# Order of the closing stage of an encoder layer: residuals, reciprocals, splits and closing sums of the output projection

## The chip, the cores and the metric

The kernel runs on one core of one Trainium2 chip. A core has five engines that work from queues of their own: TensorE (PE: matmuls, and PEld: its weight loads), VectorE (DVE), ScalarE (ACT), GpSimd (POOL) and SyncE (SP, which here only issues DMAs). The metric is the device time of one execution in microseconds (us), the median of several runs.

## The reference

One encoder layer over 2048 positions of width 1024, in float32. One input projection feeds two groups: a gated linear attention (width 512, scanned in both directions) and a latent attention with dense softmax (4 heads, width 512). Both are gated, put side by side, and go through one output projection; the result is added to the scaled input and normalised:

```python
    o_a = gla_branch(g_q, g_k, g_v, g_gate, g_lr_f, g_lr_b, wg2_f, bg_f, wg2_b, bg_b, gla_norm_g)
    o_b = mla_branch(m_cq, m_ckv, m_kr, m_gate, positions, q_norm_g, w_uq, kv_norm_g, w_ukv)
    return jnp.concatenate([o_a, o_b], axis=-1) @ w_out
...
        x = layer_norm(DEEPNORM_ALPHA * x + mixed, ln_g[layer], ln_b[layer])
```

## The kernel before

Every matrix product is made of three matmuls (`mm3`, L149 to L151): each operand is split into a high part (`hi`, L117, an ACT copy into the rounded type) and a low part (`lo`, L123, the difference, on VectorE or POOL); high times high, high times low and low times high are added up in PSUM.

The last stages are the dense attention and the output projection. The attention works through 16 blocks, 4 heads times 4 groups of 512 queries. A block ends with its row sums: `tot` brings them to SBUF, `tsum` transposes them on TensorE into a PSUM tile `sx` (L1103), `rcp` makes reciprocals `rc` of [128, 4], `keep` stores these to DRAM (`r_s`, L1115, a DMA from ACT's queue, one 4-byte element at a time), `oh` and `ol` split the block's output `o` into `ofh` and `ofl`, `y` multiplies it by the value weights, and `yc` stores that (`ob_s`). Only the last block (15) concerns us: its closing steps lie inside the output projection.

The output projection has 16 chunks of 128 positions. For a chunk c:

- `load`: four DMAs on SP of 256 KB each: the first group's half `of[:, 0]`, the gates `gr[:, 0]` (`gm_s`), the reciprocals broadcast over the partitions `gr[:, 1]` (`r_s`, L1309), and the second group's half `of[:, 1]` (`ob_s`, L1310). `load_res` fetches the residual input `xr` (512 KB, L1329).
- `split`: `hi` and `lo` of half 0 (tiles `oh`, `ol`), `gate` (two POOL multiplications of `of[:, 1]`, L1316), then `hi` and `lo` of half 1.
- `product`: two halves n of 512 output columns, each 8 steps k of three matmuls (24 matmuls); steps 0 to 3 use split half 0, steps 4 to 7 half 1. An odd chunk's two halves go into one PSUM tile of two banks (`po`, two such tiles in turn). An even chunk from 2 on has two tiles of one bank, `pmb` and `px`, one of each in the whole kernel; `px` takes its bank in turn with `sx` and `y`.
- `residual` of half n on VectorE: `rr` = alpha times `xr` plus the PSUM half (L1360), then its statistics (L1361). `finish`: mean and variance (L1369, L1370), a multiplication (L1372), the inverse root with two tiny ACT steps (`ln_l`, `ln_y`, L160 and L161) and four tiny VectorE steps (`ln_t`, `ln_r`, L162 to L165), a last multiplication (L1375), and the stores of the two halves to the output (L1376).

Dependencies are tracked by tile: a matmul into the second bank of `po` waits for a read of its first bank that was traced before it.

What sets the order: up to chunk 3's first work a list of places written out by hand orders all five engines (`in_order`, the dictionary `last`). For the rest, the loop over chunks 4 to 15 traces `load(c + 2)`, `split(c + 1)`, `load_res(c + 1)`, `product(c)` and `finish(c)`. There only SP keeps the traced order (`sp_order`, `SP_ONLY`), and the splits are only held behind the ends of the hand-written part (`ends`); the planner of the framework orders the other engines by its own costs. In the kernel before it put up to eleven matmuls of the following even chunk between an odd chunk's two halves (none in chunk 15), and splits of a chunk ahead of the ln steps of the chunk two before it. Each DMA also waits for the one eight places before it among all DMAs of SP and ACT, by its semaphore.

Of the kernel before, what the change touches and what calls it, by code (L numbers as in the profile page):

```python
# [18 lines left out]
P = 128  # L19
# [18 lines left out]
LATE_GATES = (NCH - 1, NCH - 2, 0)  # L38
STORE_POOL = (0, 1)
ENGINES = tuple(getattr(mybir.EngineType, n) for n in ("PE", "Activation", "DVE", "Pool", "SP"))  # L40
SP_ONLY = ENGINES[-1:]
RND = 1.5 * 2.0 ** 23


# [20 lines left out]
    tot=11.2,  # L65
    tsum=12.04,
    rcp=13.55,
    keep=14.21,
    oh=12.34,
    ol=12.99,  # L70
    y=16.55,
    yc=16.9,
# [36 lines left out]
class K:  # L109
# [856 lines left out]
    def attention(self):  # L966
        tc, nc = self.tc, self.nc
        mm = nc.tensor.matmul
        V, G, Ac = nc.vector, nc.gpsimd, nc.scalar
        NP = NKT // 2  # L970
        with ExitStack() as ctx:
# [6 lines left out]
            nb = len(blocks)  # L978
            stt = [dict(s=[None] * NP) for _ in blocks]
# [130 lines left out]
                V.reciprocal(rc, rc)  # L1110
                d["rc"] = rc

            def keep(i):
                h, b = blocks[i]
                Ac.dma_start(self.r_s[b][:, h].rearrange("o (e p) -> p (o e)", p=P), stt[i]["rc"])  # L1115

            def oh(i):
                d = stt[i]
# [30 lines left out]
            op = OutProj(self, ctx, qp, bp, sp, pS, pM, pX)  # L1149
# [8 lines left out]
            def at(f, i, j=None):  # L1158
                p = PLACE_LAST.get(f, PLACE[f]) if i == nb - 1 else PLACE[f]
                return p[j] if isinstance(p, tuple) else p  # L1160

            own = (("tot", tot), ("tsum", tsum), ("rcp", rcp), ("keep", keep), ("oh", oh), ("ol", ol), ("y", y), ("yc", yc))
            for i in range(nb):
                for j in range(NP):
# [42 lines left out]
            last = {}  # L1207
            for _, _, fn, a in sorted(todo, key=lambda e: e[:2]):
                with self.in_order(last):
                    fn(*a)  # L1210
            ends = [i for e, i in last.items() if e not in (mybir.EngineType.PE, mybir.EngineType.DVE)]


            late = dict(last)
            sp_order = lambda: self.in_order(late, SP_ONLY)
            rest = {c: o for c, o in enumerate(first)}

            def load(c):
                if c < NCH:
                    rest[c] = dict(c=c)  # L1220
                    op.load(rest[c])

            def split(c):
                if c < NCH:
                    with self.after(*ends):
                        for j in range(2):
                            op.hi(rest[c], j)
                            op.lo(rest[c], j)
                            if j == 0:
                                op.gate(rest[c])  # L1230

            with sp_order():
                load(4)
                for c in (2, 3):
                    op.load_res(rest[c])
                load(5)
                for c in (0, 1):
                    op.finish(rest[c])
                split(4)
                op.load_res(rest[4])  # L1240
                for c in (2, 3):
                    op.residual(rest[c], 0)
                    op.residual(rest[c], 1)
                    op.finish(rest[c])
            for c in range(4, NCH):
                with sp_order():
                    load(c + 2)
                    split(c + 1)
                    if c + 1 < NCH:
                        op.load_res(rest[c + 1])  # L1250
                    op.product(rest[c])
                    op.finish(rest[c])
                with self.after(*last.values()), sp_order():
                    for f in {4: (tot, tsum), 5: (rcp, keep, oh, ol), 6: (y,), 7: (yc,)}.get(c, ()):
                        f(nb - 1)


class OutProj:
# [88 lines left out]
    def product(self, o):  # L1347
        for n in range(2):
            for k in range(NK):
                self.part(o, k, (n,))  # L1350
            self.residual(o, n)


    def residual(self, o, n):
# [90 lines left out]
```

## Time and profile before

| | us |
|---|---|
| median of three runs | 1397.35 |
| the runs | 1395.38 to 1397.39 |
| the profiled execution | 1396.22 |
| its span, first to last instruction | 1394.4 |
| TensorE busy in the span | 1318.6 (95%) |
| VectorE busy | 1012.8 (73%) |
| ScalarE busy | 825.9 (59%) |
| GpSimd busy | 725.1 (52%) |

The page's second part cuts the span into 40 slices of 34.9 us, with the busy share in tenths. A row in order of time has the start, the duration, the engine, the line, the operation and the tiles; in square brackets stands the idle time ahead of it and what ended it. Matmuls are pipelined: a row's duration is longer than the step to the next row. A row of groups has a count behind `x`, busy time, mean, and the idle time before. `SPq` and `ACTq` are the queues in which DMAs are issued; "to landing" is the time from a DMA's issue to the arrival of its data.

### The profile page before, as it was taken

To read this page: it belongs to the slowest core of one execution; us is meant where nothing else is said; L and a number is where in the kernel's file an instruction comes from. 1 tells how busy PE (TensorE), PEld (TensorE's weight loads), DVE (VectorE), ACT (ScalarE), POOL (GpSimd) and SP (SyncE) were. 2 spreads that over 40 slices of the span, in tenths; PEclk is the share of its full clock that TensorE was granted. 3 is DMA by queue.
4 is the path that set the end of the run, shared out by engine and by line. 5 is a ranking of instruction groups with operands and counts; after the bars stand their busy time and mean duration, and the time that the engine had idled before them with its cause. 6 is when DMAs were issued, how large, how long until landed. Compare 5 with 4: busy or idle time off the path is not lost.

```text
span 1394.4 us, 19845 instructions
## 1 busy us (share of the span) xinstructions
PE 1318.6 (95%) x7056; PEld 1141.4 (82%) x7056; DVE 1012.8 (73%) x1829; ACT 825.9 (59%) x1353; POOL 725.1 (52%) x394
## 2 busy tenths in 40 slices
PE   7899999999989999999999999999999999988997
PEld 6799999999878888888778888888888887766775
DVE  7757755545598777777598888888888888384675
ACT  6655556555565555555487878788888887311110
POOL 3532423232342222221087888889999999734441
PEclk9999999999999999999999999999999999999999
DMA  7222223222565555552701111111133112465452
GB/s 248 80 74 64 68 69 91 69 69 68 179 236 165 169 179 167 167 167 93 224 0 39 39 38 38 39 53 61 54 84 84 45 31 34 141 192 161 162 187 100
DMA packets 108915, 147.38 MB, mean 106 GB/s; under 512 B 17838, under 2 KB 63278, under 8 KB 108816
## 3 DMA queue, kind: packets, MB, share of 16 engines
q1 hardware_dynamic: 99696, 143.98, 34.1%
q0 software_dynamic: 672, 2.10, 0.4%
q10 hardware_dynamic: 8448, 0.03, 0.3%
q8 instruction: 56, 0.92, 0.3%
q14 instruction: 43, 0.35, 0.1%
HBM read 94.93 MB, written 51.15 MB: 105 GB/s over the span
## 4 chain that ended last, share of the span: by engine, by line
PE 44%; DVE 12%; DMA 6%; ACT 3%; issue 2%; SPq 1%; POOL 1%; DVEq 0%; POOLq 0%; ACTq 0%
PE o L149 4%; PE o L150 4%; PE o L151 4%; PE pS L1000 4%; PE pS L1003 4%; PE pS L1002 4%; PE pS L1004 4%; PE pS L1001 4%; DMA xr<-x_dram 2%; DVE MMb L123 2%; DMA of<-ob_s 1%; PE po L149 1%; PE po L150 1%; PE ipm L149 1%; PE po L151 1%
## 5 line engine op out<-in xcount | busy, mean ns | idle before, releaser
L123 POOL TENSOR_TENSOR pl<-s,ph 128x1024 fp32r<-128x1024 f32 x128 | 307.1, 2414 | 66.9 <-ACT ph L117 60.4
L1022 DVE TENSOR_TENSOR rm<-pS,rm 128x512 f32<-128x512 f32 x210 | 144.9, 690 | 44.5 <-ACT s L1009 39.4
L1009 ACT ACTIVATE s<-pS 128x1024 f32<-128x1024 f32 x128 | 131.3, 1027 | 67.4 <-PE pS L1004 64.9
L1046 DVE TENSOR_TENSOR s<-s,mb 128x1024 f32<-128x1024 f32 x128 | 151.2, 1213 | 9.2 <-PE mb L1040 9.2
L117 ACT ACTIVATE ph<-s 128x1024 fp32r<-128x1024 f32 x128 | 135.1, 1057 | 16.7 <-PE o L151 16.1
L1050 ACT ACTIVATE s<-s 128x1024 f32<-128x1024 f32 x128 | 131.4, 1050 | 13.5 <-DVE s L1046 13.4
L149 PE MATMUL ipa<-wah,xah 128*128 128x384 f32 (+1 forms) x384 | 130.9, 341 | 6.0 <-ACT wah L117 6.0
L151 PE MATMUL ipa<-wah,xal 128*128 128x384 f32 (+1 forms) x384 | 126.1, 328 | 0.0
L150 PE MATMUL ipa<-wal,xah 128*128 128x384 f32 (+1 forms) x384 | 125.5, 327 | 0.2 <-DVE wal L123 0.2
L645 POOL TENSOR_TENSOR Us<-Us,cw 128x512 f32<-128x512 f32 x16 | 18.2, 1137 | 199.4 <-DVE Us L642 170.1
L1000 PE MATMUL pS<-qh,ckvT_h 128*128 128x512 f32 x256 | 103.9, 406 | 2.6 <-ACT s L1009 1.9
L149 PE MATMUL o<-ph,vh 128*128 128x512 f32 x256 | 102.6, 401 | 0.0
L151 PE MATMUL o<-ph,vl 128*128 128x512 f32 x256 | 101.3, 396 | 0.0
L1003 PE MATMUL pS<-rh,krs 128*128 128x512 f32 x256 | 101.2, 395 | 0.0
L150 PE MATMUL o<-pl,vh 128*128 128x512 f32 x256 | 101.1, 395 | 0.0
L1002 PE MATMUL pS<-qh,ckvT_l 128*128 128x512 f32 x256 | 100.8, 394 | 0.0
L1004 PE MATMUL pS<-rl,krs 128*128 128x512 f32 x256 | 100.7, 393 | 0.0
L1001 PE MATMUL pS<-ql,ckvT_h 128*128 128x512 f32 x256 | 100.7, 393 | 0.0
L117 ACT ACTIVATE oh<-of 128x512 fp32r<-128x512 f32 x32 | 20.0, 629 | 126.6 <-POOL of L1316 92.4
L1073 DVE TENSOR_TENSOR ap<-ap,s 128x512 f32<-128x512 f32 x120 | 83.1, 692 | 6.4 <-ACT s L1050 4.5
L149 PEld LDWEIGHTS ipa<-wah,xah 128*128 128x128 f32 x384 | 73.7, 192 | 6.8 <-ACT wah L117 6.0
L150 PEld LDWEIGHTS ipa<-wal,xah 128*128 128x128 f32 x384 | 74.0, 193 | 1.3 <-DVE wal L123 0.6
(319 smaller groups left out, 3932.0 us busy)
## 6 DMA issues: line engine op xcount, KB each, us to landing
xcf<-xT_dram SPq DMA_DIRECT2D x16, 512.0 KB, 4.3
xr<-x_dram SPq DMA_DIRECT2D x16, 512.0 KB, 5.5
out_dram<-rr SPq DMA_DIRECT2D x32, 256.0 KB, 2.0
xaf<-xT_dram SPq DMA_DIRECT2D x14, 512.0 KB, 4.2
SU<-su_s SPq DMA_DIRECT2D x16, 256.0 KB, 3.6
qdb<-qd_s SPq DMA_DIRECT2D x16, 256.0 KB, 4.2
oib<-oi_s SPq DMA_DIRECT2D x16, 256.0 KB, 2.7
ub<-u_s SPq DMA_DIRECT2D x16, 256.0 KB, 3.0
```

The costliest lines, as they stand in the source:

```text
L117: return nc.scalar.activation(dst, src, AF.Copy).ins
L123: return e.tensor_tensor(dst, src, hi.bitcast(F32), ALU.subtract).ins
L149: mm(out, ah, bh, start=start, stop=False)
L150: mm(out, ah, bl, start=False, stop=False)
L151: mm(out, al, bh, start=False, stop=stop)
L1000: mm(ps[:, e], kh, qh, start=True, stop=False)
L1001: mm(ps[:, e], kh, ql, start=False, stop=False)
L1002: mm(ps[:, e], kl, qh, start=False, stop=False)
L1003: mm(ps[:, e], kr, rh, start=False, stop=False)
L1004: mm(ps[:, e], kr, rl, start=False, stop=True)
L1022: V.tensor_tensor(d["rm"], src[:, e], d["rm"], ALU.max)
L1046: V.tensor_tensor(s, s, d["mb"][:, None, :].to_broadcast([P, 2, QB]), ALU.subtract)
```

## The change

Four things change in the output projection:

- In an odd chunk both residuals are traced behind both halves. Even chunks stay as they were.
- The order of ACT, POOL and SP is the traced one from the hand-written part to the end (`LATE_ORDER`); the splits are no longer held behind `ends`.
- The last block's closing steps are traced elsewhere: `tot`, `oh`, `ol` after chunk 4, `tsum` and `rcp` after chunk 5, `y` and `yc` after chunk 7.
- The last block's reciprocals are stored in four DMAs of 128 elements, after chunks 6, 7, 8 and 9. The other blocks' stores stay whole.

```diff
-SP_ONLY = ENGINES[-1:]
+LATE_ORDER = ENGINES[1], ENGINES[3], ENGINES[4]
...
-            def keep(i):
+            def keep(i, e=None):
                 h, b = blocks[i]
-                Ac.dma_start(self.r_s[b][:, h].rearrange("o (e p) -> p (o e)", p=P), stt[i]["rc"])
+                es = slice(0, 4) if e is None else slice(e, e + 1)
+                Ac.dma_start(self.r_s[b][:, h].rearrange("o (e p) -> p (o e)", p=P)[:, es], stt[i]["rc"][:, es])
...
-            ends = [i for e, i in last.items() if e not in (mybir.EngineType.PE, mybir.EngineType.DVE)]
...
-            sp_order = lambda: self.in_order(late, SP_ONLY)
+            fixed = lambda: self.in_order(late, LATE_ORDER)
...
             def split(c):
                 if c < NCH:
-                    with self.after(*ends):
-                        for j in range(2):
-                            op.hi(rest[c], j)
-                            op.lo(rest[c], j)
-                            if j == 0:
-                                op.gate(rest[c])
+                    op.hi(rest[c], 0)
+                    op.lo(rest[c], 0)
+                    op.gate(rest[c])
+                    op.hi(rest[c], 1)
+                    op.lo(rest[c], 1)
...
-                with self.after(*last.values()), sp_order():
-                    for f in {4: (tot, tsum), 5: (rcp, keep, oh, ol), 6: (y,), 7: (yc,)}.get(c, ()):
+                with self.after(*last.values()), fixed():
+                    for f in {4: (tot, oh, ol), 5: (tsum, rcp), 7: (y, yc)}.get(c, ()):
                         f(nb - 1)
+                    if 6 <= c < 10:
+                        keep(nb - 1, c - 6)
...
         for n in range(2):
             for k in range(NK):
                 self.part(o, k, (n,))
-            self.residual(o, n)
+            if o["c"] % 2 == 0:
+                self.residual(o, n)
+        if o["c"] % 2:
+            self.residual(o, 0)
+            self.residual(o, 1)
```

In the changed program TensorE does the two halves of an odd chunk without other matmuls between them, `sx` behind chunk 5 and `y` behind chunk 7; ACT does, from chunk 4 on, the two splits of chunk c + 1, then the ln steps of chunk c.

More of the change, by code (lines that the diff above doesn't have):

```diff
@@ L1224, in split @@
                 if c < NCH:
-                    with self.after(*ends):
-                        for j in range(2):
-                            op.hi(rest[c], j)
-                            op.lo(rest[c], j)
-                            if j == 0:
-                                op.gate(rest[c])
-            with sp_order():
+                    op.hi(rest[c], 0)
[3 more added lines that the diff above has]
+                    op.lo(rest[c], 1)
+            with fixed():
                 load(4)
@@ L1245, in attention @@
             for c in range(4, NCH):
-                with sp_order():
+                with fixed():
                     load(c + 2)
```

## The prediction

> **What bounds the kernel now.** I read the page first (busy shares, the 40 slices), then TensorE's rows in order of time from the last attention product to the end, then the waits, the DMA landings and the other engines' rows around TensorE's gaps.
>
> ```profile
> PE 1318.6 (95%) x7056; PEld 1141.4 (82%) x7056; DVE 1012.8 (73%) x1829; ACT 825.9 (59%) x1353; POOL 725.1 (52%) x394
> PE   7899999999989999999999999999999999988997
> ```
>
> TensorE is the bound of the whole run; what is left to win in the last five slices, where the change works, is its gaps. All gaps from output chunk 4 on, and some rows around them:
>
> ```profile
> 1227.31 0.39 PE L151 MATMUL po<-woh,ol 128*128 128x512 f32 x1
> 1229.78 0.47 PE L149 MATMUL pmb<-woh,oh 128*128 128x512 f32 x1 [2.09 <-DVE rr L1360]
> ...
> 1234.20 0.39 PE L149 MATMUL pmb<-woh,oh 128*128 128x512 f32 x1
> ...
> 1245.15 0.66 PE L1103 MATMUL sx<-ident,acc 128*128 128x128 f32 x4 [1.69 <-DVE rr L1360]
> ...
> 1259.79 0.80 PE L149 MATMUL po<-woh,oh 128*128 128x512 f32 x1 [6.65 <-DVE rr L1360]
> ...
> 1264.94 0.40 PE L149 MATMUL po<-woh,oh 128*128 128x512 f32 x1
> ...
> 1270.66 0.39 PE L149 MATMUL px<-woh,oh 128*128 128x512 f32 x1
> ...
> 1275.87 0.39 PE L151 MATMUL px<-woh,ol 128*128 128x512 f32 x1
> ...
> 1284.32 0.50 PE L149 MATMUL po<-woh,oh 128*128 128x512 f32 x1 [0.84 <-DVE rr L1360]
> ...
> 1289.67 0.39 PE L151 MATMUL po<-woh,ol 128*128 128x512 f32 x1
> ...
> 1308.65 0.50 PE L149 MATMUL po<-woh,oh 128*128 128x512 f32 x1 [2.27 <-DVE rr L1360]
> ...
> 1312.63 0.40 PE L150 MATMUL po<-wol,oh 128*128 128x512 f32 x1
> ...
> 1333.99 0.50 PE L149 MATMUL po<-woh,oh 128*128 128x512 f32 x1 [1.65 <-DVE rr L1360]
> ...
> 1357.80 0.50 PE L149 MATMUL po<-woh,oh 128*128 128x512 f32 x1 [1.74 <-DVE rr L1360]
> ...
> 1380.16 0.50 PE L149 MATMUL po<-woh,oh 128*128 128x512 f32 x1 [1.20 <-DVE rr L1360]
> ```
>
> There are eight gaps, and each ends on VectorE's residual (L1360). Six stand before a po matmul: the second half of chunks 5, 7, 9, 11, 13, 15, which waits until VectorE has read the first half of the same two-bank tile. Matmuls follow at (1275.87 - 1270.66) / 23 = 0.2265 us, though a row lasts 0.39; so a gap loses its listed idle time plus 0.16. A half-chunk (24 matmuls) takes 5.44 us, a chunk 10.87.
>
> **The change part by part.**
>
> *Residuals of odd chunks behind both halves.* The second half no longer waits. The six po gaps go: 6.65 + 0.84 + 2.27 + 1.65 + 1.74 + 1.20 = 14.35 listed. At the end of the run the first half's residual and statistics of chunk 15 now lie on the path, which they did not. An even chunk that did both at once shows their price:
>
> ```profile
> 1372.94 0.68 DVE L1360 SCALAR_TENSOR_TENSOR rr<-xr,pmb 128x512 f32<-128x512 f32 x1
> ...
> 1375.70 0.21 DVE L1369 BATCH_NORM_AGGREGATE mv<-bn 128x2 f32<-128x12 f32 x1
> ...
> 1385.95 0.69 DVE L1360 SCALAR_TENSOR_TENSOR rr<-xr,po 128x512 f32<-128x512 f32 x1 [5.11 <-PE po L151]
> ...
> 1387.40 0.21 DVE L1369 BATCH_NORM_AGGREGATE mv<-bn 128x2 f32<-128x12 f32 x1
> ```
>
> 2.76 us against 1.45: the tail grows by 1.31.
>
> *Closing sums later.* The transposes of the row sums (sx, L1103) stand in the middle of chunk 5's first half and wait 1.69 for VectorE to free their bank, which chunk 4's px holds. In the changed order they come after all of chunk 5, where that read is most of a chunk past: 1.69 goes. The product y, three matmuls, moves from chunk 7's first half to behind chunk 7; same work. The split ofh/ofl of the last block moves behind chunk 4's finish and takes 0.55 off VectorE ahead of chunk 2's residual (two starts below).
>
> *One order for ACT, POOL and SP.* ACT now runs the ln pair of chunk 1 ahead of the splits oh of chunk 4, where it stood behind them, and so on for each chunk. VectorE waited for it:
>
> ```profile
> 1221.50 0.63 DVE L123 TENSOR_TENSOR ofl<-o,ofh 128x512 fp32r<-128x512 f32 x1
> 1222.05 1.40 DVE L1375 SCALAR_TENSOR_TENSOR rr<-rr,ln_r,lnb 128x512 f32<-128x512 f32 x2
> ...
> 1228.05 1.00 DVE L162 TENSOR_TENSOR ln_t<-ln_y 128x1 f32<-128x1 f32 x1 [2.17 <-ACT ln_y L161]
> ...
> 1239.93 0.15 DVE L1370 TENSOR_SCALAR u<-mv 128x1 f32<-128x1 f32 x1
> ```
>
> Without the 2.17 and the 0.55, chunk 2's residual, which follows the row at 1228.05 and released chunk 4's first matmul, is done 2.7 us sooner: the gap of 2.09 at 1229.78 goes.
>
> Against this stands a new wait. ACT now does the splits of chunk 5 after the ln of chunk 3, and so after its u (1239.93 here), which in VectorE's new order has chunk 4's first residual ahead of it (0.6). u comes at 1239.93 - 2.17 - 0.55 + 0.6 = 1237.8. From u to the last split of chunk 5: ln 0.45, oh 0.63, ol 1.26, two gates 2.62, oh 0.63, ol 1.26, some 0.3 of hand-overs, 7.2 in all (rows below): done at 1245.0. TensorE without gaps starts chunk 5 at 1227.54 + 10.87 = 1238.4 and wants that split 14 matmuls later, at 1241.6. That is a wait of 3.4 at most; nothing at best, if VectorE, with the splits out of its way, closes up its 1228-1239 stretch by as much again. Between the ends I take 2.
>
> *Steps behind each other in the later chunks.* SP stays in order: chunk 10's loads stand behind chunk 7's stores. Nothing more is added to a queue than the three extra store parts on ACT (one issue each). The chain as it ran:
>
> ```profile
> 1297.95 1.00 SPq L1376 DMA_DIRECT2D out_dram<-rr  x2
> 1301.22 0.52 SPq L1310 DMA_DIRECT2D of<-ob_s  x1
> 1306.73 2.62 POOL L1316 TENSOR_TENSOR of<-of,gr 128x512 f32<-128x512 f32 x2 [2.16 <-DMA of<-ob_s]
> 1309.38 0.63 ACT L117 ACTIVATE oh<-of 128x512 fp32r<-128x512 f32 x1 [5.86 <-POOL of L1316]
> 1310.09 2.51 POOL L123 TENSOR_TENSOR ol<-of,oh 128x512 fp32r<-128x512 f32 x2 [0.74 <-ACT oh L117]
> ```
>
> Chunk 7 ended on TensorE at 1289.9; chunk 10's last split was done at 1311.4, that is 21.5 later. Without gaps TensorE wants it at 2 x 10.87 + 3.17 = 24.9 after chunk 7's end. Slack 3.4, or 2.1 with the odd chunk's finish 1.3 later: the loads stay hidden, cost nothing. If that cover goes, every us beyond it is TensorE's.
>
> *Reciprocals stored in four parts.* In the trace the whole store (512 elements of 4 bytes) sits in the worst place:
>
> ```profile
> DMA to landing us min/median/max: 8.2/8.3/9.2
> ...
> SPq L1309 <- DMA r_s<-rc: 6.2, 1, 6.2
> ...
> xr<-x_dram SPq DMA_DIRECT2D x1, 512.0 KB, 11.7
> of<-ob_s SPq DMA_DIRECT2D x1, 256.0 KB, 11.3
> ...
> of<-ob_s SPq DMA_DIRECT2D x13, 256.0 KB, 6.5
> ```
>
> (Landing of the reciprocal stores; SP's wait for one; chunk 5's residual input and chunk 6's ob load, issued in the same 0.7 us; the median of such loads.) SP stood 6.2 us for this store and the two loads beside it took 11 us instead of 6; the 6.65 us gap waited for that xr. With the store moved behind chunks 6 to 9 and cut in four, this place is free. A part is bounded by a quarter, 2.1, and the whole, 8.3; I take 3.7, a little over the quarter, as a load also has some fixed time. It delays its neighbours by at most 11.3 - 6.5 = 4.8 if it acts like the whole, by 1.2 if like a quarter; the latter stays inside the slack.
>
> *TensorE's clock.* After three of the gaps the matmuls run slowly: 12 steps from 1229.78 to 1234.20 take 4.42 where 2.72 is usual, 12 from 1259.79 to 1264.94 take 5.15, ten from 1308.65 to 1312.63 take 3.98 for 2.27. Excess 1.70 + 2.43 + 1.71 = 5.84, after waits of 2.09, 6.65 and 2.27; after 1.74 and less, none. I take it that the excess goes with the waits. The Trainium skill (TensorE: Matmul & The Clock Gate, "Why this matters for your kernels") puts the limit at idle gaps of about 3 us. By that rule two of the three stretches would have another cause and stay, and the sum would be smaller by 1.70 + 1.71 = 3.41. The rows speak for the shorter limit.
>
> *The sum*, against the profiled execution: gaps 2.09 + 1.69 + 14.35 = 18.13, plus 8 x 0.16 = 1.28, plus clock 5.84: 25.25 won. Lost: tail 1.31; the new wait in chunk 5, with 1.7 of clock once it passes about 2: between 0 and 3.4 + 1.7 = 5.1, of which I take 2.9, a wait of 2 with half the clock's loss, since 2 lies between the waits of 1.74 and 2.09. Net 21.0. The execution took 1396.2 us around a span of 1394.4, 1.1 below the median of 1397.35. From the median: 1376.3, and I say 1376.
>
> **The rivals.**
>
> *The parts act like whole stores.* For: the store's length comes from its small packets, and four collide with four loads instead of one. Against: a quarter of the packets. Four chunks would be late by 4.8 - 3.4 = 1.4: 1376 + 5.6 = 1382.
>
> *The clock does not come back* in the two stretches after waits of 2.09 and 2.27, because something other than the wait sets it: 1376 + 3.4 = 1379. For: a wait of 1.74, after which nothing is slow, is hardly shorter than these. Against: no other stretch is slow without such a wait before it. This is what the page's limit of about 3 us would make of it.
>
> *The loads become the bound in part.* TensorE now asks for a chunk's seven transfers of 256 and 512 KB in 10.9 us instead of 12, and loads slow each other. If each of the ten chunks from 6 on waits 1.1: 1387. For: two loads in the crowded stretch took 11 us. Against: a median of 6.5 and 3.4 of slack.
>
> *Slower.* ACT's fixed order makes a ring: the stores of chunk 7, the loads of 10 behind them, its gates, its last oh, and the ln of chunk 9 behind that oh, without which the stores of 9 cannot go. The ln part, at chunk 14:
>
> ```profile
> 1376.13 0.20 ACT L160 ACTIVATE ln_l<-u 128x1 f32<-128x1 f32 x1 [6.19 <-DVE u L1370]
> 1376.36 0.20 ACT L161 ACTIVATE ln_y<-ln_l 128x1 f32<-128x1 f32 x1
> ...
> 1377.33 0.15 DVE L162 TENSOR_TENSOR ln_t<-ln_y 128x1 f32<-128x1 f32 x1
> ...
> 1377.90 0.16 DVE L165 TENSOR_TENSOR ln_r<-ln_y,ln_t 128x1 f32<-128x1 f32 x1
> 1378.10 1.41 DVE L1375 SCALAR_TENSOR_TENSOR rr<-rr,ln_r,lnb 128x512 f32<-128x512 f32 x2
> ```
>
> As the ring ran, from 1297.95 to the end of that oh at 1310.0 is 12.1; with ln 0.45, ln_t 0.8 and the first L1375 0.7 it is 14.0 per two chunks, against 21.7 on TensorE. The two chunks of before took (1380.16 - 1259.79) / 5 = 24.1. The ring decides from a landing 7.7 longer (5.5 as it ran, so over 13 us), and makes the kernel slower once a pair takes 21.7 + 21/5 = 26, a landing 12 longer. At 27 per pair five pairs lose 26: 1376 + 26 = 1402. Against: one load in the trace came near 12 us, beside the store that moves.
>
> *No change.* The gaps go and as much waiting for splits comes: 1397. Only if the ring runs at 24.
>
> **How the numbers follow.** Forecast 0.63 (its own range 1371 to 1381: new wait 0 to 5.1, the runs' spread of 2); parts like whole stores 0.10; clock stays 0.08; loads in part 0.10; slower 0.05; no change 0.04. Faster by over 0.2% (2.8 us, about what a measurement of this kernel can tell): 0.91; within: 0.04; slower: 0.05. The range 1370 to 1388 leaves out the last two and the edge of the others.
>
> **What would show it.** Right: no TensorE gap before the second half of an odd chunk; pairs of chunks of 21.8 us; one gap of 1 to 4 us near the middle of chunk 5's first half, ended by POOL's split or ACT; about 2.8 us from the last residual's start to the last aggregate; no SP wait for the reciprocals. Wrong: matmuls of later chunks waiting for ol or oh, load landings over 10 us near a reciprocal part, or slow matmuls without a gap before them.

## The result, and the profile after

| | before | changed |
|---|---|---|
| median, us | 1397.37 (4 runs, 1395.38 to 1399.83) | 1374.97 (4 runs, 1374.48 to 1379.36) |
| ratio | | 0.9846, 95% interval 0.9820 to 0.9871 |
| the profiled execution / its span, us | 1396.22 / 1394.4 | 1379.36 / 1377.5 |

The changed kernel is faster by 22.4 us, between 18 and 25 by the interval; the prediction said 1376 in 1370 to 1388. The profiled execution of the changed kernel is the slowest of its four (the others' spans are 1372.6 to 1373.4), so single rows are compared stage by stage below, not end to end.

In the changed file the lines behind the diff stand 4 further down: the residual is L1364, the statistics L1365, the aggregate L1373, the last multiplication L1379, the output stores L1380. First TensorE's rows in order of time, changed kernel: chunk 4's first matmul, every gap after it, and the last matmul.

```profile
1228.73 0.39 PE L151 MATMUL po<-woh,ol 128*128 128x512 f32 x1
1228.95 0.39 PE L149 MATMUL pmb<-woh,oh 128*128 128x512 f32 x1
...
1240.95 0.50 PE L151 MATMUL po<-woh,ol 128*128 128x512 f32 x1 [0.50 <-POOL ol L123]
...
1244.22 0.50 PE L149 MATMUL po<-woh,oh 128*128 128x512 f32 x1 [0.69 <-ACT oh L117]
...
1245.57 0.50 PE L151 MATMUL po<-woh,ol 128*128 128x512 f32 x1 [0.62 <-POOL ol L123]
...
1257.11 0.50 PE L149 MATMUL pmb<-woh,oh 128*128 128x512 f32 x1 [0.32 <-ACT oh L117]
...
1258.47 0.50 PE L151 MATMUL pmb<-woh,ol 128*128 128x512 f32 x1 [0.62 <-POOL ol L123]
...
1325.37 0.50 PE L151 MATMUL pmb<-woh,ol 128*128 128x512 f32 x1 [0.57 <-POOL ol L123]
...
1337.00 0.50 PE L149 MATMUL po<-woh,oh 128*128 128x512 f32 x1 [0.91 <-ACT oh L117]
...
1338.36 0.50 PE L151 MATMUL po<-woh,ol 128*128 128x512 f32 x1 [0.62 <-POOL ol L123]
...
1367.73 0.39 PE L151 MATMUL po<-woh,ol 128*128 128x512 f32 x1
```

No gap ends on VectorE any more. What is left, 4.85 us in eight waits, ends on the splits: 1.81 in chunk 5, 0.94 in chunk 6, and 2.10 in chunks 12 and 13, where nothing was expected. No matmul is slow behind any of them: the granted clock, the share of its full speed that TensorE was let run at, is 1.00 from 1195 us to the last matmul.

The account of the two profiled executions: from chunk 3's last matmul to chunk 15's last, before 1385.53 - 1227.31 = 158.2, changed 1367.73 - 1228.73 = 139.0: 19.2 won. From there to the end of the span 8.9 before, 9.8 now: 0.9 lost. And chunk 3 ended 1.4 later; so much later this execution was already at 1196 us, ahead of what the change reorders. 19.2 - 0.9 - 1.4 = 16.9, the difference of the spans. Below, "the stage" is the time from the first matmul of chunk 4 to the last of chunk 15: 155.8 before, 138.8 now. It is the sharper measure: where chunk 4 starts differs between the profiled executions of these kernels by up to 8 us (1224.4 to 1232.8). Much of that goes with the clock ahead of the stage: the traces have five stretches of 3.41 us at half the granted clock ahead of the earliest start, nine ahead of the latest, and seven in each of the two executions above.

VectorE at the end, and the landings: the four parts of the store, and the residual inputs issued between 1262 and 1320 us, changed kernel.

```profile
1368.16 1.28 DVE L1364 SCALAR_TENSOR_TENSOR rr<-xr,po 128x512 f32<-128x512 f32 x2 [4.63 <-PE po L151]
1369.36 1.28 DVE L1365 BATCH_NORM_STATS2 bn<-rr 128x6 f32<-128x512 f32 x2
1370.67 0.21 DVE L1373 BATCH_NORM_AGGREGATE mv<-bn 128x2 f32<-128x12 f32 x1
...
DMA to landing us min/median/max: 8.3/11.0/12.9
DMA to landing us min/median/max: 6.1/6.7/12.3
```

From the first residual to the aggregate 2.51 us. A part of 128 elements lands after 8.3 to 12.9 us, and a residual input beside it after 12.3. That is about as long as a whole store takes in this stage. The 8.2 to 9.2 of the kernel before are the stores of blocks 0 to 14, in the attention; for block 15's the trace has no landing, but SP's wait for it ended at 1259.11, 12.3 us after its issue at 1246.77.

### The profile page after: what moved, and what is told of

It reads as the page before. It is cut to its first block, busy times and chain, and to the rows that moved or that the text cites. A ratio compares the mean times of both kernels' runs of the same rounds, so it can differ in the third digit from the quotient of the medians.

```text
span 1377.5 us, 19847 instructions
## 1 busy us (share of the span) xinstructions
PE 1312.2 (95%) x7056; PEld 1137.9 (83%) x7056; DVE 1013.1 (74%) x1829; ACT 826.2 (60%) x1353; POOL 727.1 (53%) x394
## 4 chain that ended last, share of the span: by engine, by line
PE 50%; DVE 8%; issue 4%; ACT 3%; POOL 2%; DMA 2%; SPq 1%; DVEq 0%; POOLq 0%; ACTq 0%
PE o L149 4%; PE o L151 4%; PE o L150 4%; PE pS L1000 4%; PE pS L1003 4%; PE pS L1002 4%; PE pS L1004 4%; PE pS L1001 4%; PE po L151 1%; PE po L150 1%; PE po L149 1%; DVE MMb L123 1%; PE ipm L149 1%; PE ipm L150 1%; PE ipm L151 1%
## 5 line engine op out<-in xcount | busy, mean ns | idle before, releaser
L1050 ACT ACTIVATE s<-s 128x1024 f32<-128x1024 f32 x128 | 131.4, 1050 | 13.5 <-DVE s L1046 13.4
L123 POOL TENSOR_TENSOR ol<-of,oh 128x512 fp32r<-128x512 f32 x32 | 43.6, 1361 | 68.8 <-ACT oh L117 58.8
```

The lines of the kernel that those rows point to most:

```text
L123: return e.tensor_tensor(dst, src, hi.bitcast(F32), ALU.subtract).ins
```

## The experiments

The change's parts are named R (residuals of odd chunks behind both halves), O (the written order of ACT, POOL and SP) and S (closing sums and the store in parts elsewhere). All ratios are to the kernel before on the same chip.

| kernel | ratio (95%) | stage, us | TensorE waits listed from chunk 4 on, us |
|---|---|---|---|
| before | 1 | 155.8 | 18.1 |
| R alone | 0.9929 (0.9903 to 0.9955) | 141.9 | 7.6 |
| O alone | 1.0004 (0.9995 to 1.0013) | 159.6 | 19.8 |
| O and S, R undone | 1.0131 (1.0110 to 1.0153) | 178.0 | 33.8 |
| R and S, O undone | 0.9913 (0.9890 to 0.9936) | 142.4 | 8.1 |
| R and O, S undone | 0.9869 (0.9846 to 0.9893) | 141.6 | 6.1 |
| changed | 0.9846 (0.9820 to 0.9871) | 138.8 | 4.9 |
| changed, again on another chip | 0.9846 (0.9822 to 0.9870) | 137.8 | 4.1 |
| store whole, behind chunk 6 | 0.9828 (0.9808 to 0.9848) | 135.8 | 2.7 |
| store as four rows | 0.9833 (0.9811 to 0.9856) | 137.2 | 3.8 |
| chunk 15 in single banks | 0.9860 (0.9837 to 0.9882) | 138.4 | 4.5 |
| rows, and chunk 5's splits ahead | 0.9808 (0.9791 to 0.9825) | 132.9 | 0.6 |
| the same with chunk 15 in single banks | 0.9804 (0.9787 to 0.9821) | 134.4 | 1.6 |

(The kernel before has 2.09 more ahead of its stage, R alone 1.61, R and S 1.81: the gap in front of chunk 4 is listed in the last column but ends where the stage begins.)

**R alone.** `product` of the changed kernel in the kernel before:

```diff
             for k in range(NK):
                 self.part(o, k, (n,))
-            self.residual(o, n)
+            if o["c"] % 2 == 0:
+                self.residual(o, n)
+        if o["c"] % 2:
+            self.residual(o, 0)
+            self.residual(o, 1)
```

> The kernel before with the residuals of odd chunks put behind both halves and nothing else. Theory of the prediction: the six gaps before second halves go (14.35 us listed and 0.16 each), and the slow matmuls behind the gaps of 6.65 and 2.27 (4.1 us); the tail grows by about 1.1; the gaps of 2.09 and 1.69 in chunks 4 and 5 stay, and SP's wait of 6.2 us for the reciprocals stays but is hidden. Net 18 us: about 1379. Rival: the store of the reciprocals still holds chunk 8's loads up, which TensorE now wants sooner, and some 4 us of waiting for splits comes back: about 1383.

Measured 1386.68 against 1397.34 beside it, 8 us less gain than expected. The six gaps are gone, but the closing sums, still in their old places, wait longer. TensorE's rows:

```profile
1230.80 0.47 PE L149 MATMUL pmb<-woh,oh 128*128 128x512 f32 x1 [1.61 <-DVE rr L1364]
...
1246.19 1.08 PE L1103 MATMUL sx<-ident,acc 128*128 128x128 f32 x4 [3.32 <-DVE rr L1364]
...
1273.27 0.55 PE L149 MATMUL y<-ofh,wv_h 128*128 128x512 f32 x1 [2.39 <-DVE rr L1364]
```

`sx` and `y` take the bank of `px` in the first half of an odd chunk. TensorE now arrives there before VectorE has read chunk 4's and chunk 6's `px`: 3.32 in place of 1.69, and 2.39 where there was nothing, each with slow matmuls behind it (12 steps from `y` on take 4.44 us in place of 2.72). Neither theory had this: waiting for splits did not come back, but for one wait of 0.31 in chunk 6.

**O and S, R undone**: the edit above taken out of the changed kernel.

> The changed kernel with the residuals of odd chunks back between the halves. Theory: six gaps before second halves come back, all of 0.8 to 2.3 us, since the input of chunk 5's residual no longer lands beside the store: some 9 us listed, 1 us of restarts and up to 1.7 us of slow matmuls, less 1.1 us of tail and less part of the waits for splits, which have more time: 8 to 11 us over the changed kernel, about 1384. Rival: the first gap keeps its 6.65 us and its slow matmuls, because something other than the store made it late: about 1391.

Measured 1415.45, slower than before by 1.3%: far outside both expectations. Rows of SP, ACT and TensorE in order of time:

```profile
1268.01 2.04 SPq L1376 DMA_DIRECT2D out_dram<-rr  x2
1270.14 0.38 SPq L1307 DMA_DIRECT2D of<-oa_s  x1
...
1272.31 0.34 ACTq L1116 DMA_DIRECT2D r_s<-rc  x1
...
1282.31 0.63 ACT L117 ACTIVATE oh<-of 128x512 fp32r<-128x512 f32 x1 [9.80 <-DMA of<-oa_s]
...
1283.00 0.80 PE L149 MATMUL pmb<-woh,oh 128*128 128x512 f32 x1 [8.06 <-ACT oh L117]
...
1288.63 0.80 PE L149 MATMUL po<-woh,oh 128*128 128x512 f32 x1 [4.84 <-DVE rr L1360]
...
1322.86 0.79 PE L149 MATMUL po<-woh,oh 128*128 128x512 f32 x1 [7.85 <-DVE rr L1360]
```

This is a ring. Chunk 8's loads stand behind chunk 5's stores on SP (1268.01), so they are issued at 1270.14. The first part of the store follows 2 us later, and chunk 8's first load is there only at 1282.3, 12 us after its issue. TensorE waits 8.06 for its split. Chunk 7's and 9's first-half residuals need their `xr` in the middle of the chunk, 5.4 us earlier than with R, and the inputs land late too (up to 13.5 us between 1255 and 1330): 4.84 and 7.85. Each wait makes the next stores, and so the next loads, later.

The written order and the residuals between the halves are not enough for this ring: O alone, further down, has both, and its stage takes 159.6 us. What comes on top here is S. The first three of chunk 8's loads, issued from 1270.14 to 1273.03, land after 12.1 to 12.8 us, and the part of the store issued at 1272.31 after 10.1. That the parts do it, and not the moved closing sums, is read from these rows; no run separates the two.

**R and S, O undone.** The changed kernel with the planner's order of ACT and POOL:

```diff
-            fixed = lambda: self.in_order(late, LATE_ORDER)
+            sp_order = lambda: self.in_order(late, SP_ONLY)
...
+                    with self.after(*ends):
+                        for j in range(2):
+                            op.hi(rest[c], j)
+                            op.lo(rest[c], j)
+                            if j == 0:
+                                op.gate(rest[c])
```

> The changed kernel with the scheduler's order on ACT and POOL in place of the written one. Theory: VectorE waits for ACT's ln of chunk 1 again, so the gap of 2.09 us before chunk 4 comes back with 1.7 us of slow matmuls behind it, and the three short waits in chunk 5 (2.3 us with restarts) go: 1 to 3 us over the changed kernel, about 1377. Rival: the scheduler's order lets the splits run early in every chunk, so that the waits of chunks 6, 12 and 13 go as well: 1 to 3 us under it, about 1373.

Measured 1384.89: 9 us above the changed kernel's ratio, not 1 to 3. Two of TensorE's waits and an ACT row:

```profile
1231.81 0.47 PE L149 MATMUL pmb<-woh,oh 128*128 128x512 f32 x1 [1.81 <-DVE rr L1367]
...
1258.19 0.50 PE L149 MATMUL pmb<-woh,oh 128*128 128x512 f32 x1 [1.20 <-ACT oh L117]
...
1300.40 0.63 ACT L117 ACTIVATE oh<-of 128x512 fp32r<-128x512 f32 x1 [7.58 <-DMA of<-oa_s]
```

Chunk 4's gap is back, as expected, though with 1.81 and no slow matmuls behind it. Besides, every even chunk from 6 to 14 waits for its splits (1.82, 1.50, 0.97, 1.34, 0.62), the other way round than the rival had it. ACT's splits wait for their loads there. R alone, with the same planner, has one such wait, of 0.31. Why the loads come later with S was not separated from the planner's other choices. One of them is that it issued all four parts of the store together (1264.39 to 1266.2), so that this run does not spread them over chunks 6 to 9 as the changed kernel does.

**R and O, S undone.** In the changed kernel:

```diff
-                    for f in {4: (tot, oh, ol), 5: (tsum, rcp), 7: (y, yc)}.get(c, ()):
+                    for f in {4: (tot, tsum), 5: (rcp, keep, oh, ol), 6: (y,), 7: (yc,)}.get(c, ()):
                         f(nb - 1)
-                    if 6 <= c < 10:
-                        keep(nb - 1, c - 6)
```

> The changed kernel with the closing sums, the last block's splits, its product and the whole store of the reciprocals in their old places. Theory: the wait of the transposes (1.7 us with restart 1.9) comes back; the store makes SP wait 6 us again, chunk 5's residual input lands late, and, since ACT now runs in one order, the ln of chunk 5 holds up the splits of chunk 7: 2 to 4 us there. About 1379. Rival: with the residuals behind both halves nothing waits for that store any more: 1376.5.

Measured 1379.22, the expected number for another reason:

```profile
1244.49 1.11 PE L1103 MATMUL sx<-ident,acc 128*128 128x128 f32 x4 [4.99 <-DVE rr L1362]
...
1284.60 0.50 PE L151 MATMUL pmb<-woh,ol 128*128 128x512 f32 x1 [0.62 <-POOL ol L123]
```

The transposes alone wait 4.99, not 1.69, with slow matmuls behind them. Chunk 7 waits for nothing, and from chunk 9 to the end there is no wait, where the changed kernel has 2.10 us in chunks 12 and 13. The stage is 2.8 us longer than the changed kernel's; the intervals of the two ratios overlap.

**O alone.** The kernel before with `LATE_ORDER` and its `split`, nothing else.

> The kernel before with the written order on ACT, POOL and SP and nothing else: residuals between the halves, closing sums and whole store in their old places. By the prediction's steps the order alone wins the gap of 2.09 us and the slow matmuls behind it: about 1393.5. Theory now, from the run with the residuals undone (1415): in the written order the ln of a chunk stands behind the splits of the next, VectorE's multiplies behind that ln, and the next first-half residual behind those, so that with residuals between the halves TensorE's second half waits for splits and loads in a ring: slower than before, 1402 to 1412.

Measured 1399.57 against 1398.93: no difference, and so between the two theories. Chunk 4's gap of 2.09 goes and the gap of 6.65 shrinks to 0.38, but five others grow. TensorE's rows:

```profile
1246.11 1.12 PE L1103 MATMUL sx<-ident,acc 128*128 128x128 f32 x4 [4.99 <-DVE rr L1358]
...
1282.14 0.79 PE L149 MATMUL po<-woh,oh 128*128 128x512 f32 x1 [3.94 <-DVE rr L1358]
...
1333.33 0.50 PE L149 MATMUL po<-woh,oh 128*128 128x512 f32 x1 [3.00 <-DVE rr L1358]
...
1360.03 0.50 PE L149 MATMUL po<-woh,oh 128*128 128x512 f32 x1 [3.03 <-DVE rr L1358]
```

They were 1.69, 0.84, 1.65 and 1.74. So the written order costs as much at the closing sums and the odd chunks' middles as it wins elsewhere, unless R takes these waits away. With R it is worth 0.006 to 0.007 of the ratio, some 9 us; without R nothing.

**The store.** Two kernels: one whole store behind chunk 6, and the reciprocals turned on TensorE and stored as four rows.

```diff
-                    if 6 <= c < 10:
-                        keep(nb - 1, c - 6)
+                    if c == 6:
+                        keep(nb - 1)
```

> The changed kernel with the four parts of the reciprocal store put back into one store behind chunk 6. In the changed kernel the parts land after 8 to 13 us each and the DMA engines move 148 to 207 GB/s beside them, at a busy share over 1.0, where they move 260 to 280 elsewhere. Theory now: a store this small costs its neighbours the same whatever part of it is sent, so three of four such stretches go, with the waits for splits in chunks 12 and 13 (2.1 us listed, 2.6 with restarts): 1.5 to 3 us under the changed kernel, about 1373. Rival, the prediction's: a part costs a quarter, the whole holds chunk 8's or 9's loads 5 us longer than the slack: 1 to 3 us over it.

```diff
+            def turn(i):
+                d = stt[i]
+                t = pX.tile([P, 4, P], F32, tag="x", name=f"rt{i}")
+                nc.tensor.transpose(t[0:4, 0], d["rc"], self.ident)
+                d["rw"] = bp.tile([P, 2, QB], F32, tag="acc", name=f"rw{i}", bufs=1)
+                V.tensor_copy(d["rw"][0:4, 0, 0:P], t[0:4, 0])
+                h, b = blocks[i]
+                Ac.dma_start(self.r_s[b][:, h].rearrange("o (e p) -> (o e) p", p=P), d["rw"][0:4, 0, 0:P])
...
-                    if 6 <= c < 10:
-                        keep(nb - 1, c - 6)
+                    if c == 6:
+                        turn(nb - 1)
```

> The changed kernel with the reciprocals transposed on TensorE behind chunk 6 and stored once, as four rows of 512 bytes in place of 512 elements of 4 bytes. Theory: the landing falls from 8 to 13 us to under 4, no load beside it passes 8 us, and the waits of chunks 12 and 13 go: about 1372.5, at or slightly under the whole store. Rival: what is slow is the landing behind the loads in the same DMA engines, whatever the layout: landing 8 us or more still, loads over 10 beside it, and the time is that of the whole store.

Measured 0.9828 and 0.9833: under the changed kernel, but within its interval. The rows are clearer. The whole store's landing, and the landing of the residual inputs issued from 1262 to 1320 beside it:

```profile
DMA to landing us min/median/max: 10.8/10.8/10.8
DMA to landing us min/median/max: 6.9/7.0/7.0
```

The same of all transfers with the reciprocals, the store among them, from 1255 to 1320, and of the residual inputs, for the four rows:

```profile
DMA to landing us min/median/max: 5.0/5.2/6.4
DMA to landing us min/median/max: 6.0/6.5/6.9
```

The ten microseconds from 1270 on, by windows, in the order parts, whole, rows (the last two numbers are the DMA engines' busy share and the GB/s they moved):

```profile
1270.00:1280.00 10.00, 10.00 (x46) 8.23 (x45) 5.07 (x9) 0.63 (x1) 5.03 (x4) 1.00 1.01 162
```

```profile
1270.00:1280.00 10.00, 10.00 (x45) 8.26 (x44) 4.02 (x9) 0.92 (x3) 4.20 (x3) 1.00 0.92 129
```

```profile
1270.00:1280.00 10.00, 10.00 (x46) 8.23 (x45) 5.62 (x13) 2.05 (x5) 5.11 (x5) 1.00 0.62 207
```

Beside a store of single elements the engines are busy more than twice as long for each byte (1.01 at 162 and 0.92 at 129, against 0.62 at 207; the rows' own store was issued at 1265.29, and from 1265 to 1272 the share beside it is 0.83 at 267 GB/s), and for about as long whether it is a quarter or the whole: one part of 128 elements landed after 11.9 us (issued at 1268.65), the whole of 512 after 10.8. Four parts make four such stretches (the third weaker, 0.76 at 186 from 1292 to 1303), the whole one, the rows none. In both kernels the waits of chunks 12 and 13 are gone. The theory that a part is cheap falls, and it is the layout that is slow: the rows land with the loads, within 6.4. That this landing is under 4, as expected, isn't shown: the trace has no row for it alone. The Trainium skill (DMA: Bandwidth & Descriptors, "Rules for kernel authors") says of many small transfers that they are to be made one large one; these landings agree (one store of 10.8 us in place of four of 8.3 to 12.9).

**Chunk 15 in single banks.**

```diff
-        if c < 2 or c % 2:
+        if c < 2 or (c % 2 and c < NCH - 1):
...
-            if o["c"] % 2 == 0:
+            if o["c"] % 2 == 0 or o["c"] == NCH - 1:
                 self.residual(o, n)
-        if o["c"] % 2:
+        if o["c"] % 2 and o["c"] < NCH - 1:
```

> The changed kernel with chunk 15 in the two single banks that even chunks use, and its first residual back between the halves. Theory: the second half doesn't wait, since nothing shares its bank, and the last residual is followed by the aggregate after 1.45 us in place of 2.51: 1.1 us under the changed kernel, about 1374. Rival: chunk 14's residual in px has not been read when chunk 15's second half wants the bank, and the wait takes the gain: no difference.

Measured 0.9860, not told from the changed kernel's 0.9846. From the last matmul to the end of the span some 8.7 us in place of 9.8, and a new wait takes half of it:

```profile
1355.90 0.68 DVE L1364 SCALAR_TENSOR_TENSOR rr<-xr,pmb 128x512 f32<-128x512 f32 x1
...
1356.72 0.47 PE L149 MATMUL pmb<-woh,oh 128*128 128x512 f32 x1 [0.48 <-DVE rr L1364]
```

**Waits of several lengths.** In chunks 7 to 15 the first residual is between the halves again, followed by none, one, two, three and no further reads (the copies go to a place that the second residual overwrites):

```diff
             if o["c"] % 2 == 0:
                 self.residual(o, n)
+            elif n == 0 and o["c"] >= 7:
+                self.residual(o, 0)
+                for _ in range((0, 1, 2, 3, 0)[(o["c"] - 7) // 2]):
+                    self.nc.vector.tensor_copy(o["rr"][:, 1], o["ps"][0])
```

> The changed kernel with the first half's residual of chunks 7, 9, 11, 13 and 15 back between the halves, followed in 9, 11 and 13 by one, two and three more reads of that half by VectorE (0.65 us each), so that TensorE waits some 1.2 us in 7 and 15 and up to 2, 2.6 and 3.3 us in 9, 11 and 13. Theory of the prediction: from a wait of about 2 us on, the next 12 matmuls take 4.4 us in place of 2.7, below it none is slow. Rival, a limit of about 3 us: only the longest wait, if any, is followed by slow matmuls.

It did not make the waits that it was meant to: one execution of 1420.66, with

```profile
1282.56 0.80 PE L149 MATMUL po<-woh,oh 128*128 128x512 f32 x1 [8.51 <-DVE rr L1369]
...
1403.02 0.50 PE L149 MATMUL po<-woh,oh 128*128 128x512 f32 x1 [3.57 <-DVE rr L1369]
```

and others of 7.44, 2.83 and 3.86, because the first-half residuals come late in the middle of a chunk, as in the run with R undone (VectorE sat idle 7.24 us before chunk 7's). Those of 2.83 and 3.86 end on a split of the following even chunk, whose matmuls the planner put between the halves. All five are followed by slow matmuls; between 0.9 and 2.8 this run has no wait. Other runs have some (last section).

**A version meant to be better than both.** The rows' store moved behind chunk 9, and chunk 6's loads, chunk 5's splits and its residual input ahead of chunk 3's finish:

```diff
                 for c in (2, 3):
                     op.residual(rest[c], 0)
                     op.residual(rest[c], 1)
+                    if c == 3:
+                        load(6)
+                        split(5)
+                        op.load_res(rest[5])
                     op.finish(rest[c])
             for c in range(4, NCH):
                 with fixed():
-                    load(c + 2)
-                    split(c + 1)
-                    if c + 1 < NCH:
-                        op.load_res(rest[c + 1])
+                    if c > 4:
+                        load(c + 2)
+                        split(c + 1)
+                        if c + 1 < NCH:
+                            op.load_res(rest[c + 1])
...
+                    if c == 9:
+                        turn(nb - 1)
```

> The changed kernel itself, to stand beside the two versions of this chip: 1375 to 1378, ratio 0.983 to 0.987, and the waits of chunks 12 and 13 there again, since every execution has the four parts among its loads.

> The changed kernel with the reciprocals transposed and stored as four rows behind chunk 9, and the loads of chunk 6, the splits of chunk 5 and the input of its residual put ahead of chunk 3's finish in the written order. Theory: the splits of chunk 5 no longer stand behind the ln of chunk 3, so its three waits go (1.8 to 2.0 us listed, 2.3 to 2.5 with restarts); the loads of chunk 6 no longer stand behind chunk 3's stores, so its waits go (0.6 to 1.2); those of chunks 12 and 13 go with the element-wise parts (about 2.5). From chunk 4's first matmul to the last one 131.6 to 133 us in place of 138.8; 4 to 6 us under the changed kernel, about 1370. Rival: the ln of chunk 3, now behind those splits, holds VectorE and with it the residual that frees chunk 6's bank, and one wait is exchanged for another: 2 us under it at most.

> The version before this one in the list, with chunk 15 in single banks and its first residual back between the halves. In the run of that edit alone the tail was 1.1 us shorter, but chunk 15 waited 0.48 us for a residual that was late. Theory: that residual was late because of loads held up beside the parts, so the wait goes and 1.0 us of tail is left as gain. Rival: it is late by VectorE's own order, and the gain is 0.4 us, which these rounds can hardly tell.

On one chip, against 1398.93 of the kernel before: changed 1377.19, this version 1372.75, with single banks 1370.96. In this execution of the changed kernel chunk 12 waits again (0.66 and 0.62), chunk 13 does not, though both were expected to. All gaps of the version without single banks from chunk 4 on, with its first and last matmul:

```profile
1229.78 0.39 PE L149 MATMUL pmb<-woh,oh 128*128 128x512 f32 x1
...
1255.54 0.50 PE L151 MATMUL pmb<-woh,ol 128*128 128x512 f32 x1 [0.21 <-POOL ol L123]
...
1267.10 0.50 PE L151 MATMUL po<-woh,ol 128*128 128x512 f32 x1 [0.39 <-POOL ol L123]
...
1362.65 0.39 PE L151 MATMUL po<-woh,ol 128*128 128x512 f32 x1
```

The three waits of chunk 5 are gone, so they came from the ln of chunk 3 ahead of its splits. The stage takes 132.9, the expected 131.6 to 133, 4.9 less than the changed kernel's in the same session; the medians differ by 4.4, and the two intervals of the ratio overlap a little (up to 0.9825, and from 0.9822). With single banks chunk 15 waits again (0.47 behind VectorE's residual), though no element-wise part is left: the rival, VectorE's own order, was right. The two medians are 1.8 apart, and their intervals overlap. What makes VectorE late is in its rows: a step of chunk 13's ln, then the same step of chunk 14's.

```profile
1349.05 1.14 DVE L165 TENSOR_TENSOR ln_r<-ln_y,ln_t 128x1 f32<-128x1 f32 x1
...
1357.64 0.16 DVE L165 TENSOR_TENSOR ln_r<-ln_y,ln_t 128x1 f32<-128x1 f32 x1
```

In chunk 13 three such steps take 1.25, 1.21 and 1.14 us and the last two multiplications together 2.53, while GpSimd works at chunk 15's gates and splits (1346.17 to 1352.21). In chunk 14, with GpSimd idle, they take 0.15, 0.16, 0.16 and 1.42. That is 4.2 us ahead of the residual that TensorE waits for; no run takes the one engine away to show it as the cause.

## Why the prediction was right, and where it was not

- *Residuals of odd chunks* (14.35 listed): all six gaps are gone. As a part they were not worth their gaps: R alone gave 0.9929, about 10 us, since the closing sums then wait 5.7 instead of 1.69 with two slow stretches. The prediction added the terms as if each stood alone; they hold only together.
- *Tail* (1.31): 2.51 - 1.45 = 1.06. The rows behind both halves run as two residuals, then two statistics, 1.28 a pair, where the even chunk that priced it took them in turn.
- *Closing sums* (1.69): gone. Left in place they would have cost 4.99 and a slow stretch, so the move was worth more than the trace of before showed.
- *The order, chunk 4's gap* (2.09 and 1.70 of clock): gone in every kernel with O; still there (1.61 and 1.81, without slow matmuls) where the planner's order stays.
- *The new wait in chunk 5* (2.9, between 0 and 5.1): 1.81 listed in three short waits, about 2.3 with 0.16 for each restart. None is long enough for the clock. The cause is the predicted one, as the last version shows.
- *Loads of later chunks* (cost nothing): failed. 0.32 + 0.62 in chunk 6 and 0.57 + 0.91 + 0.62 in chunks 12 and 13, 3.8 with restarts. The latter come from the next point.
- *The store in parts* (a part 3.7, neighbours delayed by 1.2, inside the slack): failed. The whole was priced at 8.3 by the stores of the attention; in this stage it takes 10.8 behind chunk 6, and took about 12.3 in the kernel before. A part lands after 8.3 to 12.9 and holds its neighbours as the whole does; SP waited 6.0 us for an `xr`. The rival that said so was right in mechanism; its price of 5.6 was too high. Putting one whole store in place of the parts shortens the stage by 138.8 - 135.8 = 3.0 (137.8 - 135.8 = 2.0 against the second execution).
- *The clock* (5.84): no slow matmul is left. That the short waits of 2.09 and 2.27 set it, and not another cause, is borne out by the runs in which such waits moved. A limit near 2 us on a single wait is not: what counts is the idle time within one step of 3.41 us (last section).
- *Slower by a ring of loads, splits and ln* (0.05): the run with R undone, 1415, shows such a ring, with landings of up to 13.5 us where the rival asked for over 13. The written order alone does not close it (O alone, 1.0004); it took S as well. In the changed kernel R leaves 5.4 us more for `xr` and the splits.
- *The signs named ahead:* two of the three for being wrong did show, waits for `oh` and `ol` in later chunks and a landing over 10 us near a part (12.3).

The sum against the stage: 25.25 - 2.9 = 22.35 was said up to chunk 15's last matmul, 19.2 was measured; the 3.1 between them are the waits of chunks 6, 12 and 13 (3.8) less what chunk 5 cost less than said (0.6). With the tail, 18.3 of the predicted 21.0 can be found in rows. The medians differ by 22.4, inside an interval of 18 to 25. Which rows hold the 4 us above 18.3 stays open: one profiled execution of each kernel can't tell it from the spread of chunk 4's start. So it is partly luck that the total, 1376 against 1374.97, came out nearer than its terms.

## What to carry to other kernels

A wait's price holds only while the waits around it stay: parts that undo each other's new waits have to be costed together, by asking at each shared bank and queue who now arrives first. Splitting a store of single elements does not make its pieces cheap; change its layout (here a transposition, and four rows) so that the bytes lie together. And where one order ties several queues together, look for the ring, and for the step that gives it slack, before a step is moved back.

## What the runs showed of the hardware that was not expected

*The clock after a wait.* Slow matmuls followed single waits of 2.09, 2.27, 2.39, 2.83, 3.00 and all from 3.23 on, and two waits of 1.20 and 0.62 0.7 us apart; none followed 1.61 to 1.88, but none followed 2.29 (R undone) and 3.03 (O alone) either. So it is no limit of length alone. The granted clock tells more: in all fourteen traces it changes only at steps of 3.41 us, which run on through the whole span. O alone's two waits of 3.00 (at 1333.33) and 3.03 (at 1360.03), cut at these steps; the first number behind the comma is TensorE's busy time, with its matmuls, and the third from the end the granted clock:

```profile
1331.23:1334.65 3.42, 1.32 (x6) 1.11 (x7) 1.38 (x2) 0.63 (x1) 2.54 (x2) 1.00 0.93 317
1334.65:1338.06 3.41, 3.41 (x10) 2.64 (x9) 0.00 (x0) 0.00 (x0) 1.28 (x1) 0.50 0.72 181
...
1355.13:1358.54 3.41, 1.87 (x9) 1.21 (x7) 2.60 (x6) 0.00 (x0) 1.24 (x2) 1.00 0.78 278
1358.54:1361.95 3.41, 1.92 (x8) 1.61 (x9) 1.38 (x2) 0.63 (x1) 2.59 (x3) 1.00 0.85 275
1361.95:1365.37 3.42, 3.42 (x16) 2.81 (x15) 0.00 (x0) 0.00 (x0) 0.70 (x1) 1.00 0.79 250
```

The first wait leaves 2.10 us of one step idle, and the next step has half the clock. The second is shared out between two steps, 1.54 and 1.49, and no step is slow. It is so in every trace. From 1198 us on, each of the 18 steps at full clock with 2.01 us or more of idle time was followed by one at half the clock, none with 1.59 or less was, and of two with 1.81 one was. A step at half the clock was followed by another where 0.59 us or more of it was idle, and not with 0.49 or less. In the changed kernel no step of the stage has over 0.94.

The Trainium skill (TensorE: Matmul & The Clock Gate, "What's actually happening") has the clock set by how busy TensorE was in a window of about 3.4 us that runs freely. The steps agree. It lets the clock fall after a window that is idle; here a little over half a window was enough.

*Small stores.* 128 elements of 4 bytes landed no sooner than 512 did (8.3 to 12.9 us, 10.8), and beside them the DMA engines were over 90% busy at 129 and 162 GB/s, where the rows' kernel moved 207 at 62%. The busy share is not the whole account: with R undone, from 1276 to 1282, the engines were 10 to 29% busy at 11 to 14 GB/s, and loads issued from 1270 on had not landed. Why is open.
